# Weighted values of an even and an odd head issued alternately, each in its own half of the TensorE columns

## The chip, the cores and the metric

The program runs on one core of a Trainium2 chip. The metric is the device time of one execution in microseconds; the kernel before was timed three times. One further execution was taken with the hardware profiler, and all rows below are from that one. TensorE is called PE in the rows (PEld is its weight load), VectorE DVE, ScalarE ACT, GpSimd POOL, and SP is the engine that issues the DMAs.

## The reference

Two layers work on 256 tokens of width 1024. Each layer normalises, projects to a wide row (queries, keys and values of four mixers, gates, merge weights), runs four causal mixers with four heads of 64 each, merges their outputs through gates, and adds one output projection. Cut to what matters here:

```python
def _hybrid_layer(x, norm_w, w_in, cmp_pos, cmp_w1, cmp_w2, w_up, w_out):
    h = _rmsnorm(x, norm_w)
    proj = jnp.einsum('bsd,dc->bsc', h, w_in)
    ...
    o_a = _moba_attention(...)             # 4 heads, causal softmax over 256 keys
    o_b = _nsa_attention(...)              # 4 heads, three branches: compressed, selected, window
    o_c = _stick_breaking_attention(...)   # 4 heads, stick-breaking weights
    o_d = _dilated_attention(...)          # 12 heads in 3 groups, combined to 4
    widened = jnp.stack([_merge_heads(o_a) * jax.nn.silu(ga), ...], axis=2)
    u = jnp.einsum('bsiw,iwd->bsid', widened, w_up)
    y = jnp.sum(jax.nn.sigmoid(merge) * u, axis=2)
    return x + y @ w_out
```

With 256 tokens, MoBA's own block and the selected and the window branch all come to full causal attention. Each head ends in the same step: a matrix of weights (256 queries by up to 256 keys) times a matrix of values (256 keys by 64).

## The kernel before

Every projection is an fp32 product made of three fp32r products (high and low parts of activations and weights), so PE runs long rows of `pp<-hh,wh`, `pp<-hl,wh`, `pp<-hh,wl` with 256 moving columns. ACT makes the high part of each half of a weight (`wh`, a cast), DVE the low part (`wl`, a subtraction); the halves arrive by DMA in five `raw` buffers, and six `wh` and `wl` buffers hold them until PE has used them.

The order of all instructions is written out by a planner at build time. It goes through a list of items (T and N: projections, W1: the compressor's hidden layer, M and U: merge gates and up-projections), and between them it puts steps of the attention generators wherever its own clock says that their operands are ready (`fill`, `when`, `my_turn`, `turn`). At most three generators are open (`MAXA`). The branches come in the order a, c, b, d (`ORDER = (0, 2, 1, 3)`), the heads of a branch 0 to 3. The order on each engine is fixed by that; on the chip every engine works strictly through its own list and waits on semaphores.

One head goes as follows. Scores (`psS`, fp32r products with all 128 rows of the array) are read by DVE, softmaxed by ACT and DVE into `p` (for d: `pd`), and `transpose_P` (line 895) transposes the weights in three 128 by 128 pieces on PE into `psT`, from where ACT or DVE copies them to a buffer of the ring `ptr` (five buffers). Then come the products of this step, `mm_PV` (line 903): values are stationary (128 rows by 64 columns), transposed weights move. An even head writes partitions 0 to 63 of `psO`, an odd head partitions 64 to 127; heads 0 and 1 use the first half of the bank, heads 2 and 3 the second. One call is a product with 256 moving columns for the first 128 keys and one with 128 for the other keys. Heads of a and c make one call, heads of d three, heads of b two and one more product of 256 columns (`vct` and `pct`, the compressed branch). These products are plain fp32: the trace shows each as two records. After head 3, `close_branch` multiplies `psO` by the gate into `wid`, and then ACT and DVE split it into `widh` and `widl` for the U items.

Other products that use a part of the array's columns are those of the W1 items: four products with 32 stationary columns each, written one behind the other to the four quarters of the partitions, fp32 with 256 moving columns (`pp<-raw,xt` and `pp<-raw,qkv`; `xt` and `qkv` are buffers lent from the same ring).

The planner's price of a matmul whose output does not begin at partition 0 is `return 0.055` (line 165), and so it has been for every product of an odd head.

Of the kernel before, what the change touches and what calls it, by code (L numbers as in the profile page):

```python
# [189 lines left out]
def kernel(ctx: ExitStack, tc: tile.TileContext, x_in, w_half, w_kvb, w_up, norm_w, pe_in,  # L190
# [46 lines left out]
    ss = sb("ss", [128, 2, 5])  # L237
    rstd = sb("rstd", [128, 2])
    ms = sb("ms", [128, 2])
    pc = sb("pc", [128, 2, 4, 32])  # L240
    sg = sb("sg", [128, 2, 12])
    kct = sb("kct", [128, 2, 16])
    junk = sb("junk", [128, 1])
# [12 lines left out]
    for t in (hh[1], hl[1]):  # L256
        blk.put(t[:, 0:4, :])
        blk.put(t[:, 4:8, :])
    ptr = Ring("ptr", 5, [128, 384])
    tm = Ring("tm", 2, [128, 2, S])  # L260
    small = Ring("small", 10, [128, 16])

# [5 lines left out]
    done = set()  # L268
# [516 lines left out]
    def cmp_branch(l, h_):  # L785
        hc = h_[0:64, 0:256]
        u = p1.get()
        t_ = u[0:64, 0:256]
        nc.scalar.activation(out=t_, in_=hc, func=AF.Square)
        vec.tensor_scalar(out=t_, in0=t_, scalar1=0.044715, scalar2=1.0, op0=ALU.mult, op1=ALU.add)  # L790
        vec.tensor_tensor(out=t_, in0=t_, in1=hc, op=ALU.mult)
        act(out=t_, in_=t_, func=AF.Tanh, scale=0.7978845608028654)
        vec.scalar_tensor_tensor(out=t_, in0=t_, scalar=1.0, in1=hc, op0=ALU.add, op1=ALU.mult)
        p1.put(h_)
        yield when(u, ring=psT)
        b = rot(psT)
        for k in range(2):
            nc.tensor.transpose(b[:, 64 * k:64 * k + 64], u[0:64, 128 * k:128 * k + 128], iden[0:64, 0:64])
        gtk = u[:, 0:32].rearrange("p (k c) -> p k c", k=2)
        gtv = u[:, 32:288].rearrange("p (k h c) -> p k h c", k=2, h=4)  # L800
        bv = b[:, 0:128].rearrange("p (k c) -> p k c", k=2)
        act(out=gtk, in_=bv[:, :, 0:16], func=AF.Copy, scale=0.5)
        act(out=gtv, in_=bv[:, :, 32:64].unsqueeze(2).to_broadcast([128, 2, 4, 32]), func=AF.Copy, scale=0.5)
        yield when(gtk, gtv, ring=psT)
        b = rot(psT)
        for k in range(2):
            mm(b[:, 0:16], w2k[:, k, :], gtk[:, k, :], start=(k == 0), stop=(k == 1))
        for k in range(2):
            mm(b[:, 64:128], gtv[:, k].rearrange("p a b -> p (a b)"), w2v[:, k, :], start=(k == 0), stop=(k == 1))
        p1.put(u)  # L810
        nc.scalar.copy(kct[0:64, 0, :], b[0:64, 0:16])
        vec.tensor_copy(kct[64:128, 1, :], b[64:128, 0:16])
        for h in range(4):
            copy_to(vct[32 * h:32 * h + 32, h, :], b[32 * h:32 * h + 32, 64:128])
        while (l, "bq") not in done:
            yield cond((l, "bq"))
        yield when(kct, vct, T_[l, "bqr"], ring=psS)
        q = T_[l, "bqr"]
        b = rot(psS)
        for tt in range(2):  # L820
            for p in range(2):
                mm(b[:, 64 * tt + 32 * p:64 * tt + 32 * p + 32], q[:, 256 * p + 128 * tt:256 * p + 128 * tt + 128],
                   kct.rearrange("p a n -> p (a n)"), start=True, stop=True)
        t = p1.get()
        tv = t[:, 0:128].rearrange("p (a h n) -> p a h n", a=2, h=4)
        t8 = t[:, 0:128].rearrange("p (g n) -> p g n", n=16)
        m1, m2 = small.get(), small.get()
        vec.tensor_tensor(out=tv, in0=b[:, 0:128].rearrange("p (a h n) -> p a h n", a=2, h=4),
                          in1=cmask[:, 0].unsqueeze(2).to_broadcast([128, 2, 4, 16]), op=ALU.add)
        vec.tensor_reduce(out=m1[:, 0:8], in_=t8, op=ALU.max, axis=mybir.AxisListType.X)  # L830
        vec.tensor_tensor(out=t8, in0=t8, in1=m1[:, 0:8].unsqueeze(2).to_broadcast([128, 8, 16]), op=ALU.subtract)
        act(out=t[:, 0:128], in_=t[:, 0:128], func=AF.Exp, scale=0.125)
        qkv.put(q)
        while (l, "bkv") not in done:
            yield cond((l, "bkv"))
        vec.tensor_tensor(out=tv, in0=tv, in1=cmask[:, 1].unsqueeze(2).to_broadcast([128, 2, 4, 16]), op=ALU.mult)
        vec.tensor_reduce(out=m1[:, 0:8], in_=t8, op=ALU.add, axis=mybir.AxisListType.X)
        vec.tensor_scalar(out=m1[:, 0:8], in0=m1[:, 0:8], scalar1=1e-30, scalar2=None, op0=ALU.max)
        vec.reciprocal(out=m2[:, 0:8], in_=m1[:, 0:8])
        m2v = m2[:, 0:8].rearrange("p (a h) -> p a h", a=2)  # L840
        vec.tensor_tensor(out=m2v, in0=m2v, in1=sg[:, :, 0:4], op=ALU.mult)
        vec.tensor_tensor(out=pc[:, :, :, 0:16], in0=tv, in1=m2v.unsqueeze(3).to_broadcast([128, 2, 4, 16]), op=ALU.mult)
        p1.put(t)
        small.put(m1)
        small.put(m2)
        yield when(pc, ring=psT)
        b = rot(psT)
        for tt in range(2):
            nc.tensor.transpose(b[:, 128 * tt:128 * tt + 128], pc[:, tt].rearrange("p h n -> p (h n)"), iden)
        nc.scalar.copy(pct, b[:, 0:256])  # L850
        done.add((l, "cmp"))

# [47 lines left out]
        copy_to(t, b[:, 0:384])  # L900
        return t

    def mm_PV(h, v0, v1, pt, start, stop):
        r, p = 64 * (h % 2), h // 2
        mm(psO[r:r + 64, p, :], v0, pt[:, 0:256], start=start, stop=False)
        mm(psO[r:r + 64, p, 128:256], v1, pt[:, 256:384], start=False, stop=stop)

    def close_branch(l, i, scale):
        vec.scalar_tensor_tensor(out=wid[i].rearrange("p a b -> p (a b)"), in0=psO.rearrange("p a b -> p (a b)"),
# [9 lines left out]
            yield cond((l, "pv", i, h))  # L919

    def finish_head(l, i, h, scale, last):
        done.add((l, "pv", i, h + 1))
        if h == 3:
            done.add((l, "pvs", i))
            gn = (l, "g" + "abcd"[i])
            while gn not in done:
                yield cond(gn)
            yield when(psO)
            close_branch(l, i, scale)
            if last is not None:  # L930
                done.add((l, "pv", last, 0))
# [3 lines left out]
    def head_a(l, h):  # L935
        q, k, v = T_[l, "aq"], T_[l, "ak"], T_[l, "av"]
        b = mm_S(q, k, h)
        if h == 3:
            blk.put(q), blk.put(k[0]), kl.put(k[1])
        p, acc = p1.get(), small.get()  # L940
        score(b, p, 0, 0, acc, True)
        softmax(p, 1, acc)
        yield my_turn((l, 0, h), 1, p)
        pt = transpose_P(p, 0)
        seq["next"] += 1
        p1.put(p)
        small.put(acc)
        yield when(pt)
        yield from turn(l, 0, h)
        mm_PV(h, vslice(v, 0, 64 * h), vslice(v, 1, 64 * h), pt, True, True)  # L950
        ptr.put(pt)
        if h == 3:
            qkv.put(v)
        yield from finish_head(l, 0, h, 1.0, NEXT[0])

    def head_b(l, h):
        q, k, v = T_[l, "bq"], T_[l, "bk"], T_[l, "bv"]
        r = 64 * (h % 2)
        ps, accs = [], []
        b = mm_S2(q, k, h)  # L960
        if h == 3:
            blk.put(q), blk.put(k)
        for s in range(2):
            p, acc = p1.get(), small.get()
            score(b[s], p, 0, 0, acc, True)
            softmax(p, 1, acc, gate=sg[:, :, 4 * (s + 1) + h])
            ps.append(p)
            accs.append(acc)
        pts = []
        for s in range(2):  # L970
            yield my_turn((l, 1, h), 2 - s, ps[s])
            pts.append(transpose_P(ps[s], 0))
            p1.put(ps[s])
            small.put(accs[s])
        seq["next"] += 1
        yield when(*pts)
        while (l, "cmp") not in done:
            yield cond((l, "cmp"))
        yield from turn(l, 1, h)
        mm(psO[r:r + 64, h // 2, :], vct[:, h, :], pct, start=True, stop=False)  # L980
        for s in range(2):

            mm_PV(h, v[:, 64 * s:64 * s + 64], v[:, 128 + 64 * s:128 + 64 * s + 64], pts[s], False, s == 1)
            ptr.put(pts[s])
        if h == 3:
            qkv.put(v)
        yield from finish_head(l, 1, h, 1.0, NEXT[1])

    def head_c(l, h):
# [19 lines left out]
        pt = transpose_P(t, 0)  # L1009
        seq["next"] += 1  # L1010
        p1.put(t)
        yield when(pt)
        yield from turn(l, 2, h)
        mm_PV(h, vslice(v, 0, 64 * h), vslice(v, 1, 64 * h), pt, True, True)
        ptr.put(pt)
        if h == 3:
            qkv.put(v)
        yield from finish_head(l, 2, h, 0.5, NEXT[2])
# [16 lines left out]
    def head_d(l, h):  # L1035
# [6 lines left out]
        seq["next"] += 1  # L1042
        pd.put(p)
        small.put(acc)
        yield when(*pts)
        yield from turn(l, 3, h)
        for g in range(3):
            v = T_[l, f"dv{g}"]
            mm_PV(h, vslice(v, 0, 64 * h), vslice(v, 1, 64 * h), pts[g], g == 0, g == 2)
            ptr.put(pts[g])  # L1050
        if h == 3:
            for g in range(3):
                qkv.put(T_[l, f"dv{g}"])
# [184 lines left out]
    with tc.manual_schedule():  # L1238
# [59 lines left out]
        for t in kl.free:  # L1298
            for e in range(2):
                nc.gpsimd.memset(t[64 - 64 * e:128 - 64 * e, e::2, :].bitcast(F32), 0.0)  # L1300
        nc.gpsimd.memset(pc, 0.0)
        nc.gpsimd.memset(kct, 0.0)
        nc.gpsimd.memset(vct, 0.0)
        h0 = 0
# [167 lines left out]
```

## Time and profile before

| what | value |
|---|---|
| median of 3 runs | 658.98 us (658.93 to 659.08) |
| the profiled execution, its own time | 659.2 us |
| its span, first to last instruction | 657.3 us |
| PE busy | 639.6 us, 97% |
| PEld busy | 606.5 us, 92% |
| DVE busy | 482.8 us, 73% |
| ACT busy | 369.4 us, 56% |
| instructions | 12885 |

The profiled execution's time is 1.9 us longer than its span. Busy time of PE is the union of its records; records overlap, since a matmul of 256 columns is given some 0.28 us and the next one starts 0.12 us after it, so the pace of PE is read from starts.

### The profile page before, as it was taken

How to read it: one execution, taken by the hardware profiler on the slowest of the kernel's cores; microseconds unless marked ns; L12 is line 12 of the kernel's file. 1: busy time of each engine (PE TensorE's matmuls, PEld its weight loads, DVE VectorE, ACT ScalarE, POOL GpSimd, SP SyncE). 2: the span in 40 equal slices, each digit the busy share in tenths (PEclk: the TensorE clock that was granted, in tenths of full speed). 3: DMA queues.
4: the chain of work that ended last, by engine and by line, in shares of the span. 5: the costliest groups of instructions: out<-in, count | busy, mean ns of one | idle time of the engine just before them, and what ended most of it. 6: DMA issues, size and time to landing. Idle time of an engine off the chain costs nothing.

```text
span 657.3 us, 12885 instructions
## 1 busy us (share of the span) xinstructions
PE 639.6 (97%) x5192; PEld 606.5 (92%) x5192; DVE 482.8 (73%) x851; ACT 369.4 (56%) x656; POOL 46.5 (7%) x58
## 2 busy tenths in 40 slices
PE   7999999999999999999999999999999999999996
PEld 6998999999999999999999889899999989999996
DVE  6777788999974664667678678888999556555773
ACT  6546634545656777445464564545464757765452
POOL 3020100121100000000001101020220000000000
PEclk7999999999999999999999999999999999999998
DMA  8933255644443444567656144556336334345811
GB/s 286 330 131 123 102 203 216 234 151 145 164 159 97 147 159 137 182 243 240 215 178 232 59 166 157 186 205 224 132 128 207 132 138 146 117 153 198 290 63 65
DMA packets 34908, 112.38 MB, mean 171 GB/s; under 512 B 4257, under 2 KB 5281, under 8 KB 34849
## 3 DMA queue, kind: packets, MB, share of 16 engines
q1 hardware_dynamic: 34560, 111.07, 49.0%
q0 software_dynamic: 144, 0.49, 0.4%
q8 instruction: 41, 0.67, 0.4%
q14 instruction: 19, 0.15, 0.1%
q10 hardware_dynamic: 144, 0.00, 0.0%
HBM read 109.94 MB, written 2.10 MB: 170 GB/s over the span
## 4 chain that ended last, share of the span: by engine, by line
PE 73%; DVE 17%; issue 4%; ACT 3%; DMA 2%; POOL 0%; SPq 0%; POOLq 0%; DVEq 0%; ACTq 0%
PE pp L149 60%; PE psO L149 7%; DVE wl L149 7%; DVE rope L149 4%; PE psT L149 3%; PE psS L149 3%; DMA raw<-w_half_dram 2%; DVE xt L149 2%; DVE hl L149 1%; ACT wh L149 1%; ACT p L149 1%; DVE pd L149 1%; DVE p L149 1%; ACT hh L149 1%; DVE hh L149 0%
## 5 line engine op out<-in xcount | busy, mean ns | idle before, releaser
L149 PE MATMUL pp<-hh,wh 128*128 128x256 f32 x1008 | 290.0, 288 | 1.5 <-DVE xt L149 1.5
L149 PE MATMUL pp<-hh,wl 128*128 128x256 f32 x1008 | 282.6, 280 | 2.3 <-DVE wl L149 2.3
L149 PE MATMUL pp<-hl,wh 128*128 128x256 f32 x1008 | 282.4, 280 | 0.0
L149 DVE TENSOR_TENSOR wl<-raw,wh 128x1024 fp32r<-128x1024 f32 (+2 forms) x198 | 232.1, 1190 | 51.2 <-ACT wh L149 50.3
L149 ACT CAST wh<-raw 128x1024 fp32r<-128x1024 f32 (+2 forms) x198 | 188.7, 978 | 51.7 <-DMA raw<-w_half_dram 28.0
L149 PEld LDWEIGHTS pp<-hh,wh 128*128 128x128 f32 x1008 | 190.0, 188 | 10.0 <-issue 6.5
L149 PEld LDWEIGHTS pp<-hh,wl 128*128 128x128 f32 x1008 | 190.0, 188 | 3.2 <-DVE wl L149 3.2
L149 PEld LDWEIGHTS pp<-hl,wh 128*128 128x128 f32 x1008 | 189.9, 188 | 0.2
L149 PE MATMUL pp<-wh,hh 128*128 128x256 f32 (+1 forms) x320 | 86.1, 289 | 1.1 <-ACT hh L149 1.1
L149 PE MATMUL pp<-wl,hh 128*128 128x256 f32 (+1 forms) x320 | 83.9, 281 | 1.4 <-DVE wl L149 1.4
L149 PE MATMUL pp<-wh,hl 128*128 128x256 f32 (+1 forms) x320 | 84.3, 284 | 0.0
L149 ACT ACTIVATE p<-p,small 128x128 f32<-128x128 f32 x96 | 40.0, 448 | 38.4 <-DVE small L149 37.7
L149 PEld LDWEIGHTS pp<-wh,hh 128*128 128x128 f32 x320 | 58.8, 193 | 2.4 <-ACT hh L149 1.6
L149 PEld LDWEIGHTS pp<-wl,hh 128*128 128x128 f32 x320 | 57.6, 188 | 1.8 <-DVE wl L149 1.8
L149 PEld LDWEIGHTS pp<-wh,hl 128*128 128x128 f32 x320 | 58.2, 191 | 0.0
L149 DVE TENSOR_TENSOR rope<-pp,sinF 32x512 f32<-32x512 f32 x72 | 49.5, 687 | 6.6 <-PE pp L149 4.0
L149 POOL TENSOR_TENSOR xt<-xt,rope 128x512 f32<-128x512 f32 x14 | 28.1, 2005 | 172.2 <-DVE xt L149 140.0
L149 PE MATMUL psO<-ptr,xt 128*64 128x256 f32 x192 | 37.7, 332 | 0.0
L149 PE MATMUL pp<-widh,wh 128*128 128x256 f32 x128 | 36.5, 285 | 0.0
L149 PE MATMUL pp<-widh,wl 128*128 128x256 f32 x128 | 35.8, 280 | 0.0
L149 PE MATMUL pp<-widl,wh 128*128 128x256 f32 x128 | 35.8, 279 | 0.0
L149 ACT COPY ptr<-psT 128x384 f32<-128x384 f32 x46 | 21.2, 477 | 24.1 <-PE psT L149 24.0
(146 smaller groups left out, 688.0 us busy)
## 6 DMA issues: line engine op xcount, KB each, us to landing
raw<-w_half_dram SPq DMA_DIRECT2D x178, 512.0 KB, 4.3
raw<-w_up_dram SPq DMA_DIRECT2D x32, 256.0 KB, 3.1
raw<-w_kvb_dram SPq DMA_DIRECT2D x4, 536.0 KB, 5.6
xt<-x_in_dram SPq DMA_DIRECT2D x4, 256.0 KB, 3.2
xt<-x_in_dram SPq DMA_DIRECT2D x2, 512.0 KB, 7.3
pd<-norm_w_dram SPq DMA_DIRECT2D x2, 512.0 KB, 6.1
x_mem<-xt SPq DMA_DIRECT2D x2, 512.0 KB, 5.2
xt<-x_mem SPq DMA_DIRECT2D x2, 512.0 KB, 5.6
```

What stands on the lines that cost most here:

```text
L149: return f(*a, **k)
```

## The change

The scores are not touched. `mm_PV` becomes a generator: the even head only leaves its list of products and its `ptr` buffers in `held`; the odd head waits until the transposed weights of both are there and then issues both lists in turns, one product of the even head (partitions 0 to 63), one of the odd (64 to 127). The products themselves, their number and their operands stay. The `ptr` buffers of both heads go back after that, the ring has six of them in place of five, and room for the sixth comes from the tile `pc`, whose values now lie in a `p1` buffer, cleared by a memset in each layer in place of one at the start.

```diff
-    pc = sb("pc", [128, 2, 4, 32])
...
-    ptr = Ring("ptr", 5, [128, 384])
+    ptr = Ring("ptr", 6, [128, 384])
...
         t = p1.get()
+        pc = t[:, 128:384].rearrange("p (a h n) -> p a h n", a=2, h=4)
+        nc.gpsimd.memset(pc[:, :, :, 16:32], 0.0)
...
-        p1.put(t)
...
             nc.tensor.transpose(b[:, 128 * tt:128 * tt + 128], pc[:, tt].rearrange("p h n -> p (h n)"), iden)
+        p1.put(t)
...
-    def mm_PV(h, v0, v1, pt, start, stop):
-        r, p = 64 * (h % 2), h // 2
-        mm(psO[r:r + 64, p, :], v0, pt[:, 0:256], start=start, stop=False)
-        mm(psO[r:r + 64, p, 128:256], v1, pt[:, 256:384], start=False, stop=stop)
+    held = {}
+
+    def pv(v0, v1, pt):
+
+        return [(0, v0, pt[:, 0:256]), (128, v1, pt[:, 256:384])]
+
+    def mm_PV(l, i, h, steps, pts):
+
+        held[l, i, h] = steps, pts
+        if h % 2 == 0:
+            return
+        a, b = held.pop((l, i, h - 1)), held.pop((l, i, h))
+        yield when(*a[1], *b[1])
+        yield from turn(l, i, h - 1)
+        n = len(a[0])
+        for k in range(n):
+            for r, (st, _) in ((0, a), (64, b)):
+                c, v, p = st[k]
+                mm(psO[r:r + 64, h // 2, c:256], v, p, start=(k == 0), stop=(k == n - 1))
+        for _, pts in (a, b):
+            for pt in pts:
+                if pt is not pct:
+                    ptr.put(pt)
...
     def finish_head(l, i, h, scale, last):
-        done.add((l, "pv", i, h + 1))
+        if h % 2:
+            done.add((l, "pv", i, h + 1))
...
-        yield when(pt)
-        yield from turn(l, 0, h)
-        mm_PV(h, vslice(v, 0, 64 * h), vslice(v, 1, 64 * h), pt, True, True)
-        ptr.put(pt)
+        yield from mm_PV(l, 0, h, pv(vslice(v, 0, 64 * h), vslice(v, 1, 64 * h), pt), [pt])
...
-        mm(psO[r:r + 64, h // 2, :], vct[:, h, :], pct, start=True, stop=False)
+        steps = [(0, vct[:, h, :], pct)]
...
+            steps += pv(v[:, 64 * s:64 * s + 64], v[:, 128 + 64 * s:128 + 64 * s + 64], pts[s])
+        yield from mm_PV(l, 1, h, steps, [pct] + pts)
...
-            mm_PV(h, vslice(v, 0, 64 * h), vslice(v, 1, 64 * h), pts[g], g == 0, g == 2)
-            ptr.put(pts[g])
+            steps += pv(vslice(v, 0, 64 * h), vslice(v, 1, 64 * h), pts[g])
+        yield from mm_PV(l, 3, h, steps, pts)
...
-        nc.gpsimd.memset(pc, 0.0)
```

Since the planner sets the order, all engines' lists change. The numbers behind the names are the buffer and the tile, and a tile's number is smaller by one after the change for what is allocated behind `pc`. On PE, in layer 0, this is the second head of branch a before, with the projection around it; the products of head 0 (`ptr0_138`) stand 45 rows higher in the list, by themselves:

```order
L149 MATMUL pp1_156<-hh0_78,wh3_105 128x256
L149 MATMUL pp1_156<-hl0_80,wh3_105 128x256
L149 MATMUL pp1_156<-hh0_78,wl3_111 128x256
L149 MATMUL psO_162<-ptr1_139,xt_77 64x256
L149 MATMUL psO_162<-ptr1_139,xt_77 64x128
L149 MATMUL pp1_156<-hh0_78,wh3_105 128x256
L149 MATMUL pp1_156<-hl0_80,wh3_105 128x256
```

At the same place of the list after the change:

```order
L149 MATMUL pp1_156<-hh0_78,wh3_104 128x256
L149 MATMUL pp1_156<-hl0_80,wh3_104 128x256
L149 MATMUL pp1_156<-hh0_78,wl3_110 128x256
L149 MATMUL psO_162<-ptr0_137,xt_77 64x256
L149 MATMUL psO_162<-ptr1_138,xt_77 64x256
L149 MATMUL psO_162<-ptr0_137,xt_77 64x128
L149 MATMUL psO_162<-ptr1_138,xt_77 64x128
L149 MATMUL pp1_156<-hh0_78,wh4_105 128x256
L149 MATMUL pp1_156<-hl0_80,wh4_105 128x256
```

The products of both heads now stand in one place and take turns, and the projection is interrupted once in place of twice.

On PE, in layer 0, this is the first head of branch d before; behind it come 57 other rows and then the six products of head 1 in the same form:

```order
L149 MATMUL psO_162<-ptr1_139,xt_77 64x256
L149 MATMUL psO_162<-ptr1_139,xt_77 64x128
L149 MATMUL psO_162<-ptr2_140,xt_77 64x256
L149 MATMUL psO_162<-ptr2_140,xt_77 64x128
L149 MATMUL psO_162<-ptr3_141,qkv0_114 64x256
L149 MATMUL psO_162<-ptr3_141,qkv0_114 64x128
```

After the change the first two heads of d stand together:

```order
L149 MATMUL psO_162<-ptr4_141,xt_77 64x256
L149 MATMUL psO_162<-ptr1_138,xt_77 64x256
L149 MATMUL psO_162<-ptr4_141,xt_77 64x128
L149 MATMUL psO_162<-ptr1_138,xt_77 64x128
L149 MATMUL psO_162<-ptr5_142,xt_77 64x256
L149 MATMUL psO_162<-ptr2_139,xt_77 64x256
L149 MATMUL psO_162<-ptr5_142,xt_77 64x128
L149 MATMUL psO_162<-ptr2_139,xt_77 64x128
L149 MATMUL psO_162<-ptr0_137,qkv0_113 64x256
L149 MATMUL psO_162<-ptr3_140,qkv0_113 64x256
L149 MATMUL psO_162<-ptr0_137,qkv0_113 64x128
L149 MATMUL psO_162<-ptr3_140,qkv0_113 64x128
```

All six `ptr` buffers are in use here, three of each head, and no weights of head 2 are transposed until these rows are through.

On DVE the list of layer 0 is almost the same as before up to the branch b, and that of layer 1 differs most where branch a ends and branch c begins. Before, the first head of c (`p14`, `p13`, its scores and scans) stands ahead of the subtractions `wl5` and `wl0` and of the closing of branch a (`wid0_82<-psO`):

```order
L149 TENSOR_TENSOR wl4_112<-raw2_99,wh4_106 128x1024
L149 TENSOR_TENSOR p14_130<-psS1_159,masks_70 128x128
L149 TENSOR_TENSOR p14_130<-psS1_159,masks_70 128x256
L149 TENSOR_SCALAR p12_128<-p14_130 128x384
L149 SCALAR_TENSOR_TENSOR p13_129<-p12_128,zero_76 128x128
L149 SCALAR_TENSOR_TENSOR p13_129<-p12_128,zero_76 128x256
L149 SCALAR_TENSOR_TENSOR p14_130<-p14_130,p13_129 128x128
L149 SCALAR_TENSOR_TENSOR p14_130<-p14_130,p13_129 128x256
L149 TENSOR_TENSOR wl5_113<-raw4_101,wh5_107 128x1024
L149 TENSOR_TENSOR wl0_108<-raw0_97,wh0_102 128x1024
L149 SCALAR_TENSOR_TENSOR wid0_82<-rope0_124,pp1_156 128x512
L149 SCALAR_TENSOR_TENSOR wid0_82<-psO_162,wid0_82 128x512
```

After the change:

```order
L149 TENSOR_TENSOR wl5_112<-raw4_100,wh5_106 128x1024
L149 SCALAR_TENSOR_TENSOR wid0_82<-rope0_123,pp1_156 128x512
L149 SCALAR_TENSOR_TENSOR wid0_82<-psO_162,wid0_82 128x512
L149 TENSOR_TENSOR wl0_107<-raw0_96,wh0_101 128x1024
L149 TENSOR_TENSOR widl_87<-wid0_82,widh_86 128x512
L149 TENSOR_TENSOR hh1_79<-qkv2_115,hh1_79 64x2x256 x2
L149 TENSOR_TENSOR wl1_108<-raw3_99,wh1_102 128x1024
L149 SCALAR_TENSOR_TENSOR wid1_83<-rope1_124,pp0_155 128x512
L149 TENSOR_TENSOR p14_129<-psS1_159,masks_70 128x128
L149 TENSOR_TENSOR p14_129<-psS1_159,masks_70 128x256
L149 TENSOR_SCALAR p12_127<-p14_129 128x384
```

The head of c has moved behind three subtractions and the closing of branch a.

## Rows read from the trace of the kernel before

**Rows 1.** The page: busy times, PE's granted clock in 40 slices, the chain by line.
```profile
PE 639.6 (97%) x5192; PEld 606.5 (92%) x5192; DVE 482.8 (73%) x851; ACT 369.4 (56%) x656; POOL 46.5 (7%) x58
PEclk7999999999999999999999999999999999999998
PE pp L149 60%; PE psO L149 7%; DVE wl L149 7%; DVE rope L149 4%; PE psT L149 3%; PE psS L149 3%; DMA raw<-w_half_dram 2%; DVE xt L149 2%; DVE hl L149 1%; ACT wh L149 1%; ACT p L149 1%; DVE pd L149 1%; DVE p L149 1%; ACT hh L149 1%; DVE hh L149 0%
```
**Rows 2.** PE's timeline around one head of a: start us, us, what.
```profile
64.06 0.28 PE L149 MATMUL pp<-hh,wl 128*128 128x256 f32 x1
64.27 0.86 PE L149 MATMUL psO<-ptr,xt 128*64 128x256 f32 x4
65.06 0.38 PE L149 MATMUL pp<-hh,wh 128*128 128x256 f32 x1
65.28 0.27 PE L149 MATMUL pp<-hl,wh 128*128 128x256 f32 x1
65.40 0.28 PE L149 MATMUL pp<-hh,wl 128*128 128x256 f32 x1
```
**Rows 3.** The chain in order of time: start us, us, what.
```profile
64.34 0.80 PE psO L149 x4
...
197.47 1.88 PE psO L149 x10
...
243.40 2.10 PE psO L149 x12
...
270.07 58.03 PE pp L149 x492
```
**Rows 4.** PE's timeline of two W1 items in a row, and the row behind.
```profile
91.89 0.40 PE L149 MATMUL pp<-raw,xt 128*32 128x256 f32 x1
...
91.91 0.40 PE L149 MATMUL pp<-raw,qkv 128*32 128x256 f32 x1
92.13 0.38 PE L149 MATMUL pp<-raw,xt 128*32 128x256 f32 x1
...
92.34 0.38 PE L149 MATMUL pp<-raw,xt 128*32 128x256 f32 x1
...
92.89 0.39 PE L149 MATMUL pp<-hh,wh 128*128 128x256 f32 x1
```
**Rows 5.** The timeline of PE's weight loads, another W1 item.
```profile
60.56 0.11 PEld L149 LDWEIGHTS pp<-raw,xt 128*32 128x32 f32 x1
...
60.61 0.11 PEld L149 LDWEIGHTS pp<-raw,qkv 128*32 128x32 f32 x1
```
**Rows 6.** The instructions on `psO`: duration ns min/median/max, first and last start.
```profile
L149 PEld LDWEIGHTS psO<-ptr,xt x192: 132/137/137, 57.7 to 589.2; 128*64 128x64 f32 x192
```
**Rows 7.** DVE's timeline where branches a and c run, in brackets the idle time.
```profile
89.28 1.23 DVE L149 TENSOR_TENSOR wl<-raw,wh 128x1024 fp32r<-128x1024 f32 x1 [1.24 <-ACT wh L149]
...
100.75 0.62 DVE L149 TENSOR_TENSOR p<-psS,masks 128x128 f32<-128x128 f32 x2 [1.04 <-PE psS L149]
...
110.05 2.08 DVE L149 TENSOR_TENSOR rope<-pp,sinF 32x512 f32<-32x512 f32 x3 [1.55 <-PE pp L149]
```
**Rows 8.** Busy us by stretch: PE, PEld, DVE, ACT, POOL, clock, DMA share, GB/s.
```profile
110.00:170.00 60.00, 58.00 (x490) 55.53 (x489) 56.98 (x94) 31.75 (x49) 11.32 (x6) 1.00 0.47 162
195.00:270.00 75.00, 75.00 (x579) 68.50 (x577) 43.60 (x85) 53.03 (x108) 0.00 (x0) 1.00 0.41 134
```
**Rows 9.** DVE's timeline among the heads of b.
```profile
212.92 1.22 DVE L149 TENSOR_TENSOR wl<-raw,wh 128x1024 fp32r<-128x1024 f32 x1
```
**Rows 10.** PE's timeline, the first use of what that subtraction made.
```profile
214.65 0.28 PE L149 MATMUL pp<-hh,wl 128*128 128x256 f32 x1
```
**Rows 11.** The copies of transposed weights: duration ns min/median/max.
```profile
L149 ACT COPY ptr<-psT x46: 460/479/487, 57.1 to 585.0; 128x384 f32<-128x384 f32 x46
...
L149 DVE COPY ptr<-psT x10: 548/558/561, 63.2 to 586.8; 128x384 f32<-128x384 f32 x10
```
**Rows 12.** PE's longest waits: us in total, times, longest.
```profile
PE pp L149 <- DVE wl L149: 3.8, 5, 1.1
```

More of the change, by code (lines that the diff above doesn't have):

```diff
@@ L957, in head_b @@
         q, k, v = T_[l, "bq"], T_[l, "bk"], T_[l, "bv"]
-        r = 64 * (h % 2)
         ps, accs = [], []
@@ L975, in head_b @@
         seq["next"] += 1
-        yield when(*pts)
         while (l, "cmp") not in done:
             yield cond((l, "cmp"))
-        yield from turn(l, 1, h)
-        mm(psO[r:r + 64, h // 2, :], vct[:, h, :], pct, start=True, stop=False)
+        steps = [(0, vct[:, h, :], pct)]
         for s in range(2):
-            mm_PV(h, v[:, 64 * s:64 * s + 64], v[:, 128 + 64 * s:128 + 64 * s + 64], pts[s], False, s == 1)
-            ptr.put(pts[s])
+            steps += pv(v[:, 64 * s:64 * s + 64], v[:, 128 + 64 * s:128 + 64 * s + 64], pts[s])
+        yield from mm_PV(l, 1, h, steps, [pct] + pts)
         if h == 3:
@@ L1011, in head_c @@
         p1.put(t)
[L1012 to L1015, printed above, removed]
+        yield from mm_PV(l, 2, h, pv(vslice(v, 0, 64 * h), vslice(v, 1, 64 * h), pt), [pt])
         if h == 3:
@@ L1044, in head_d @@
         small.put(acc)
-        yield when(*pts)
-        yield from turn(l, 3, h)
+        steps = []
         for g in range(3):
             v = T_[l, f"dv{g}"]
-            mm_PV(h, vslice(v, 0, 64 * h), vslice(v, 1, 64 * h), pts[g], g == 0, g == 2)
-            ptr.put(pts[g])
+            steps += pv(vslice(v, 0, 64 * h), vslice(v, 1, 64 * h), pts[g])
+        yield from mm_PV(l, 3, h, steps, pts)
         if h == 3:
```

## The prediction

> **What bounds the kernel now.** I read the page first [rows 1]: PE is busy for 97% of the span, its granted clock stands at the full 2.4 GHz in every slice but the first and the last, and on the chain that ended last the projections (`pp`) hold 60% and the products on `psO` 7%, which is 46 us of 657.3. DVE's groups are second, some 16% together. So I looked for two things: what a product on `psO` costs PE, and where DVE and not PE sets the pace.
>
> PE's records overlap, so I take its pace from starts. In the long undisturbed run at 270 us, 492 projection records fill 58.03 us, 0.118 us each [rows 3]. Around a head of a, the last projection record ahead starts at 64.06 and the second one behind at 65.28 [rows 2]: 1.22 us where two steps of the pace would be 0.24. **One head of a or c costs PE 0.98 us.** On the chain its products hold 0.80 us; a head of b holds 1.88 and one of d 2.10 [rows 3]. With the same surroundings b costs 0.98 + 1.08 = 2.06 us and d 0.98 + 1.30 = 2.28 us. From d less a, (2.10 - 0.80) / 2 = 0.65 us, comes the price of one product of 256 moving columns with its fellow of 128, and two thirds of that, 0.43 us, for the one of 256. So 0.33 us of each head is no product at all: it is the step into half an array and back, seen as the late first starts in [rows 2]. All heads together: 16 x 0.98 + 8 x 2.06 + 8 x 2.28 = 50.4 us.
>
> **The change part by part.** *Products in turns.* Instructions and operands stay; what can change is whether the two halves of the columns work at the same time. The kernel has a row for it. In the W1 items four products with 32 stationary columns and the same 256 moving columns start at 91.89 to 91.91, and the next four at 92.34 [rows 4]: four in 0.45 us, where one alone is 0.43 and four in a row would be 1.7. They have four different moving operands and all 128 rows, as the products here. Two halves of 64 columns are that case with two parts, so a pair should cost what one head costs now, and one head of each pair goes: 8 x 0.98 + 4 x 2.06 + 4 x 2.28 = 25.2 us.
>
> Not all of it: four side by side took 0.45 where one takes 0.43. At 0.02 us a product, with 2, 5 and 6 products in the pairs, that is 8 x 0.04 + 4 x 0.10 + 4 x 0.12 = 1.2 us; if only the start of the second is later, 0.01 us a pair, 0.1 us. I take 0.5.
>
> *Weight loads.* Each record loads 64 columns, 0.137 us at the median [rows 6], twice as many per time as now. In a W1 item eight loads, for both passes of four products, start between 60.56 and 60.61 [rows 5], and the first matmul, 0.40 us long [rows 4], runs from the start of this: loads do not wait for it, though all have the same 128 rows. I price this at nothing. The Trainium skill, "TensorE: Matmul & The Clock Gate", section Part 3: Packing small matmuls — row/col tiling, says otherwise: a weight load would overlap with a running matmul only where the row groups differ, and here they are the same. By that rule this change would give much less (the third rival below has it in numbers of this trace); the W1 rows contradict it, since their row groups are the same too.
>
> *How much of it the end of the kernel sees.* A shorter PE counts where PE sets the pace. Among a and c (50 to 110 us, and again in layer 1) PE gains 4 x 0.98 = 3.9 us a layer, but the stretch behind, 110 to 170 us, is DVE's: 56.98 of 60 us busy [rows 8], and PE's largest wait in the whole trace is for `wl` [rows 12]. That stretch only moves up as far as DVE begins it earlier. Ahead of it DVE stood idle for PE 1.04 us and 1.55 us [rows 7]; these 2.6 us can go. The 1.24 us at 89.28 wait for a cast, and it is open whether that comes earlier. So 2.6 to 3.9 us a layer remain; I take the middle, 3.2, since the cast's buffers are released partly by PE.
>
> Among b and d (195 to 270 us) PE gains 2 x 2.06 + 2 x 2.28 = 8.7 us a layer. DVE is busy for 43.60 of 75 us and ACT for 53.03 [rows 8]; in 66.3 us ACT would be at 80%, so neither becomes the bound. Here the covers are single ones: a `wl` that ends at 212.92 + 1.22 = 214.14 us [rows 9] is first used at 214.65 [rows 10], 0.51 us later, when PE will be a head of b, 2.06 us, earlier. If DVE came no earlier there, 1.55 us would be lost. The remainder is between 7.1 and 8.7 us a layer; I take 8.0, since DVE itself waits for PE in this stretch and will mostly move along.
>
> *The later wait.* The even head's products now wait for the odd head's weights too, and on PE everything behind them is queued. Between the last transposes and the products the new list has at least six projection rows, 0.7 us, for a copy of 0.48 or 0.56 us [rows 11]. Behind a subtraction of 1.22 us [rows 9] DVE's copy would end 1.1 us late, but the head of [rows 2] has the same distance in the list of before, and nothing but the step of every head stands ahead of it. Nothing, then; at two such places a layer 4 us at most, for the range.
>
> *Sixth buffer, `pc`.* The buffer frees the planner to transpose all of a pair of d. A smaller memset moves from the start into each layer's 110 to 170 us, on POOL, with 11.32 of 60 us busy [rows 8]; the rope addition behind it could come later by the length of a memset, which no row has. POOL's 48 idle us hide it. The `p1` buffer that `pc` borrows is held a little longer. Nothing for both. In layer 1 the first head of c stands later on DVE, behind subtractions that it would have to do anyway; I price that at nothing too, with 1 us either way.
>
> **Sum.** 2 x (3.2 + 8.0) - 0.5 = 21.9 us. The profiled execution took 659.2 us, 0.2 above the median of the three runs, so 637.3 for such an execution and **637.1 us** for the median.
>
> **Rivals.**
> 1. *All of it arrives* (DVE moves along everywhere, and waits for `wl` shrink in the new order): 659.0 - 25.2 + 0.1 = 633.9, perhaps 1 us less. For it: DVE's idle time ahead of 110 us is largely made by PE. Against it: 95% busy behind. Chance 0.13, for anything under 634.5.
> 2. *DVE keeps more*: nothing of a and c arrives, and b and d keep 7.1 us: 659.0 - 14.2 + 0.5 = 645.3. For it: the 110 to 170 us stretch; against it: the 2.6 us that PE made. Chance 0.14 for 641 to 648.
> 3. *The loads of the odd half wait.* Odd heads have 4 records in a and c, 10 in b, 12 in d: 8 x 4 + 4 x 10 + 4 x 12 = 120 records, each with 0.137 us outside: 16.4 us of 25.2 are lost, and with the same share of what is left arriving (21.9 of 25.2), 659.0 - 7.6 = 651.4. It is what the section named above would make of it; [rows 5] speak against it. Chance 0.03.
> 4. *The change doesn't do what it says*: halves of 64 columns take turns and don't overlap. Then only 16 steps into and out of the half array go, 16 x 0.33 = 5.3 us: 653.7. Only W1 with quarters speaks against it. Chance 0.03.
> 5. *Slower.* PE stands before a pair whose odd weights are not copied, and everything queues behind. To be slower by over 0.2% this must eat 21.9 + 1.3 us, 1.45 us at each of the 16 pairs; the worst that I made of a subtraction ahead of a copy is 1.1, at the tightest places. Chance 0.01.
>
> The forecast, 634.5 to 641, has 0.66. Its own range is that; the range for 8 in 10 takes in most of the first rival and the nearer part of the second, **633 to 644**. A difference of 0.2%, 1.3 us, is about what the runs can tell from none. Faster 0.98 (all but the fifth and a sliver), same 0.01, slower 0.01.
>
> **What would show it.** Records of `psO` start in twos, some ns apart, at the pace of one head: 0.8 us for a pair of a or c, 1.9 for b, 2.1 to 2.2 for d; on the chain `psO` falls from 7% to under 4%, and PE is busy for about 617 us. In the stretch that was 110 to 170, DVE stays over 90% busy and PE's waits for `wl` grow from 3.8 to some 5 us. Between b and d no wait of PE is over 1 us. The prediction is wrong if the second record of a pair starts 0.1 us or more behind the first, if PE waits in front of `psO`, or if DVE's stretch ends no earlier than now.

## The result, and the profile after

The changed kernel takes 638.18 us (median, 637.66 to 639.46) where the kernel before takes 658.95 in the same session: a ratio of 0.9685, 95% interval 0.967 to 0.9701. That is 20.8 us less; predicted were 637.1 us, with 633 to 644 as the range. The profiled execution took 637.66 us with a span of 635.8; that is 0.5 us below its median, and before it was 0.2 us above, so the two profiled executions lie 0.8 us further apart than the medians.

The page, its busy times and the chain by line, which answer to [rows 1]:

```profile
PE 616.4 (97%) x5192; PEld 591.8 (93%) x5192; DVE 482.2 (76%) x850; ACT 369.3 (58%) x657; POOL 46.4 (7%) x59
PE pp L149 58%; DVE wl L149 7%; DVE rope L149 4%; PE psO L149 3%; PE psT L149 3%; ACT p L149 3%; PE psS L149 3%; ACT wh L149 2%; DVE xt L149 2%; DMA raw<-w_half_dram 2%; DVE hl L149 1%; DVE p L149 1%; DVE pd L149 1%; DVE kl L149 1%; DVE qkv
```

PE has as many instructions as before and 23.2 us less busy time; `psO` has gone from 7% to 3% of the chain. PE's timeline around the first pair of a (start us, us, what), where [rows 2] had one head:

```profile
63.75 0.28 PE L149 MATMUL pp<-hh,wl 128*128 128x256 f32 x1
63.96 0.87 PE L149 MATMUL psO<-ptr,xt 128*64 128x256 f32 x8
64.76 0.39 PE L149 MATMUL pp<-hh,wh 128*128 128x256 f32 x1
64.98 0.28 PE L149 MATMUL pp<-hl,wh 128*128 128x256 f32 x1
```

Eight records stand where four stood, and the projection resumes 0.80 us after they begin, as it did behind one head (0.79 in [rows 2]). The eight start in twos, each second record 7 ns behind the first, and their weight loads keep up:

```profile
63.96 0.63 PEld L149 LDWEIGHTS psO<-ptr,xt 128*64 128x64 f32 x8
```

The chain in order of time shows the same for all three kinds; these are pairs, with the durations that single heads have in [rows 3]:

```profile
64.03 0.80 PE psO L149 x8
...
202.47 1.88 PE psO L149 x20
...
237.07 2.10 PE psO L149 x24
```

PE's waits (us in total, times, longest), beside [rows 12]:

```profile
PE pp L149 <- DVE wl L149: 4.3, 5, 1.6
PE pp L149 <- DVE xt L149: 1.7, 2, 1.0
PE psO L149 <- DVE p L149: 1.5, 1, 1.5
...
PE pp L149 <- DVE widl L149: 0.9, 2, 0.5
```

The wait for `widl` is new; the one of `psO` for `p` is on eight records at the very start and as long before the change. Busy time by stretch, as in [rows 8], shows DVE still setting the pace from 110 to 170 us:

```profile
110.00:170.00 60.00, 58.05 (x491) 55.58 (x490) 57.20 (x99) 33.84 (x52) 11.85 (x7) 1.00 0.49 166
195.00:270.00 75.00, 74.50 (x645) 70.95 (x643) 47.00 (x81) 55.73 (x109) 0.00 (x0) 1.00 0.47 159
```

Where the time was gained is read from the projection's records: their number is the same in all kernels here, so the start of the k-th tells how far PE is ahead of the kernel before. The starts in us (W1 not counted):

| record, and what ends there | before | after | ahead | gained in the stretch |
|---|---|---|---|---|
| 1200, a and c of layer 0 and the stretch behind | 188.92 | 184.72 | 4.20 | 4.20 |
| 2400, b and d of layer 0 | 358.64 | 346.79 | 11.85 | 7.65 |
| 3360, a and c of layer 1 | 505.70 | 491.56 | 14.14 | 2.29 |
| 4320, b and d of layer 1 | 645.32 | 623.76 | 21.56 | 7.42 |

### The profile page after: what moved, and what is told of

Its sections match the earlier page's. It is cut to its first block, busy times and chain, and to the rows that moved or that the text cites. A ratio compares the mean times of both kernels' runs of the same rounds, so it can differ in the third digit from the quotient of the medians.

```text
span 635.8 us, 12881 instructions
## 1 busy us (share of the span) xinstructions
PE 616.4 (97%) x5192; PEld 591.8 (93%) x5192; DVE 482.2 (76%) x850; ACT 369.3 (58%) x657; POOL 46.4 (7%) x59
## 4 chain that ended last, share of the span: by engine, by line
PE 67%; DVE 19%; ACT 6%; issue 4%; DMA 2%; POOL 0%; SPq 0%; POOLq 0%; ACTq 0%; DVEq 0%
PE pp L149 58%; DVE wl L149 7%; DVE rope L149 4%; PE psO L149 3%; PE psT L149 3%; ACT p L149 3%; PE psS L149 3%; ACT wh L149 2%; DVE xt L149 2%; DMA raw<-w_half_dram 2%; DVE hl L149 1%; DVE p L149 1%; DVE pd L149 1%; DVE kl L149 1%; DVE qkv L149 1%
## 5 line engine op out<-in xcount | busy, mean ns | idle before, releaser
L149 ACT ACTIVATE tm<-pp 128x512 f32<-128x512 f32 x32 | 19.0, 592 | 22.4 <-PE pp L149 22.4
```

The source lines that it names most:

```text
L149: return f(*a, **k)
```

## The experiments

**Even list, then odd list.** The same place and the same products, but one head behind the other:

```diff
-        for k in range(n):
-            for r, (st, _) in ((0, a), (64, b)):
+        for r, (st, _) in ((0, a), (64, b)):
+            for k in range(n):
```

> The products of a pair stay in one place of PE's list, but all of the even head stand ahead of all of the odd head. Theory (the halves work at the same time only where the matmuls of the two stand in turns, since PE starts matmuls in the order of its list): a pair costs the products of both heads, 0.65 + 0.65 us in a and c, 1.73 each in b, 1.95 each in d, and one step into the half array; that is 8 x 0.65 + 4 x 1.73 + 4 x 1.95 = 19.9 us more than with turns, less up to 0.2 us a pair where the last product of the one and the first of the other overlap and less what waits take up: 653 to 658 us. Rival (PE finds the other half's matmuls in its queue by itself, so that standing close is enough): 638 us, as with turns.

Measured: 648.56 us, ratio 0.9842 (0.9828 to 0.9856). Neither was right; half of the gain is left. PE's timeline of the first pair of b says why. In the list ten records of the even head (`vct`, then four products from `ptr`) stand ahead of the odd head's `vct`:

```profile
204.63 0.65 PE L149 MATMUL psO<-pct,vct 128*64 128x256 f32 x2
205.11 1.03 PE L149 MATMUL psO<-ptr,xt 128*64 128x256 f32 x5
205.77 0.43 PE L149 MATMUL psO<-pct,vct 128*64 128x256 f32 x1
205.98 0.38 PE L149 MATMUL psO<-ptr,xt 128*64 128x256 f32 x1
206.03 0.38 PE L149 MATMUL psO<-pct,vct 128*64 128x256 f32 x1
206.19 1.52 PE L149 MATMUL psO<-ptr,xt 128*64 128x128 f32 x10
207.64 0.73 PE L149 MATMUL psS<-hl,hh 128*128 128x256 f32 x3
```

The odd head's `vct` starts at 205.77, 6 ns after the seventh even record, with three even records still to start. In d it starts 6 ns after the ninth of twelve. So, by the starts that the profile shows, PE took up the odd half with four even records left, the one just begun and three to come: two fp32 products. It did not work strictly through its list here, as the section on the kernel before has it for every engine. The four records of a head of a lie within that, and there the pair is free without any turns. The chain of this kernel:

```profile
65.99 0.81 PE psO L149 x8
...
204.70 3.01 PE psO L149 x19
...
241.51 3.45 PE psO L149 x24
```

Against the change, 4 x (3.01 - 1.88) + 4 x (3.45 - 2.10) = 9.9 us, and 648.56 - 638.18 is 10.4.

**Both heads in the same half.** The lists and turns of the change, row for row, but the odd head writes the same partitions as the even one (prices held, so that the order stays):

```diff
-                mm(psO[r:r + 64, h // 2, c:256], v, p, start=(k == 0), stop=(k == n - 1))
...
+                u = 64 * (h // 2)
+                mm(psO[u:u + 64, r // 64, c:256], v, p, start=(k == 0 and r == 0), stop=(k == n - 1 and r == 64))
...
```

> List, turns and sizes as after the change on every engine, but both heads of a pair write to the same half of the partitions, next to each other in the bank (heads 0 and 1 below, 2 and 3 above), so that the output mixes the heads' columns; nothing is left out. Theory (what is gained is the two halves of the columns at work together): every product waits for the one ahead, 19.9 us more: 654 to 658 us, and the records of psO start 0.2 us apart in place of 7 ns. Rival (the gain is in the new order, fewer steps between full and half array, or a later place of the products): 638 to 641 us.

Measured: 657.68 us, ratio 0.9973 (0.996 to 0.9985). The theory holds, and the rival falls: the new order with half as many interruptions is worth 1 to 2 us. In the trace PE, DVE, ACT and POOL each start the same operations in the same order as in the change. Its chain:

```profile
63.93 1.44 PE psO L150 x8
...
205.22 3.61 PE psO L150 x20
...
243.31 4.04 PE psO L150 x24
```

8 x 0.64 + 4 x 1.73 + 4 x 1.94 = 19.8 us more than in the change; the medians differ by 19.5. Beside this run the lists one behind the other save 0.63, 0.60 and 0.59 us at a pair (1.44 - 0.81, 3.61 - 3.01, 4.04 - 3.45), however long the pair is. That is about the 0.65 us of the four records that were left when the odd half began.

**The parts that go with it.** The sixth `ptr` buffer with `pc` in a `p1` buffer, without the new `mm_PV`; and, in another kernel, the planner's price of an odd head's products at the full value (`return 0.055` not for `psO`).

> The kernel before with only the supporting edits: six buffers of transposed weights in place of five, and the compressed branch's weights in a borrowed buffer with a memset in each layer. Products head by head as before. Theory: no part of the gain, 658 to 660 us. Rival (the sixth buffer lets the planner issue transposes earlier and that is worth something by itself): 655 us or less.

> The kernel before with only the planner's price of an odd head's products set to that of an even head's (0.43 and 0.22 us in place of 0.055). Theory: the order changes but PE's work doesn't, 657 to 661 us. Rival (the kernel before lost time because its planner took odd heads for nearly free, and the change made that price true): a part of the 21 us comes back, 650 to 656 us.

Measured: 659.14 us, ratio 1.0004 (0.9993 to 1.0016), and 660.36 us, 1.0017 (1.0004 to 1.003). Neither has a part in the gain; the second is, if anything, 0.2% slower.

**Turns of two and of three products.** These test the reading that PE looks four records ahead (shown for two; for three the step is 3):

```diff
-        for k in range(n):
+        for k0 in range(0, n, 2):
             for r, (st, _) in ((0, a), (64, b)):
-                c, v, p = st[k]
+                for k in range(k0, min(k0 + 2, n)):
+                    c, v, p = st[k]
...
```

> The pairs take turns by two products in place of one. After the run with the heads in a row the theory is changed: PE starts a matmul for the free half while up to four records (two products of two records each) of the other half stand ahead of it, the one at work included, and no more. Two products are then no more than that: each pair costs 0.80, 1.88 and 2.10 us as with turns of one, 638 us, +-0.7. Rival (any departure from strict turns costs a part, because starts follow the list and only neighbours overlap): each further product in a row costs its 0.2 to 0.43 us somewhere, 641 to 647 us.

> Turns of three products; the pairs of a and c have two and so stand in a row, which cost nothing in the earlier run. By the changed theory the odd half of b and d starts when the third record of the even half starts, 0.48 us late, and ends as much later, with no further loss since the even half is ahead: 8 pairs x 0.5 = 4 us, less what waits take up, 640 to 642.5 us; in the records the first of the odd half 0.48 us behind the first of the even half. Rival (the look-ahead is no fixed number of records; b and d lost in the earlier run because their loads or the vct product come first): 638 us, or as with the heads in a row, 648 us.

Measured: 639.27 us, ratio 0.9685 (0.9663 to 0.9708), with two; 642.32 us, 0.9735 (0.9708 to 0.9761), with three. With two, the first odd record starts 13 ns behind the first even one, and pairs of b and d take 1.93 and 2.15 us. In b the four records ahead are then all of 256 columns, 0.86 us of work, where 0.65 us were left in the run with one list behind the other: it is the number of records that fits both, not a time. Records and products can't be told apart here, since every product is two records. With three, it starts 0.489 us behind, straight after the third even record at 0.483 and again with four left; the chain of that kernel:

```profile
64.58 0.81 PE psO L149 x8
...
203.21 2.36 PE psO L149 x17
...
238.72 2.58 PE psO L149 x19
```

That is 0.48 us more at each of eight pairs, 3.8 in all; the medians differ by 4.1 across two sessions. Against turns of two, in the same session, the pairs give 3.5 and the medians 3.05.

**Where the missing 3.6 us went.** The pairs give 25.2 us on PE (below), and 21.56 arrive. In layer 0 the whole of a and c is kept (4.20 of 3.9), in layer 1 only 2.29. There the planner opens branch c late: its last pair begins at 415.87 us, 42.9 us behind the layer's first pair, where layer 0 has 38.3. My reading is that DVE then reaches its subtractions late; PE waits longest at 475.68:

```profile
475.68 0.38 PE L149 MATMUL pp<-hh,wl 128*128 128x256 f32 x1 [1.62 <-DVE wl L149]
```

A head is opened only while the planner's clocks of ACT and DVE are less than `BACKLOG` ahead of PE's (no run shows that this is what held c back). So I raised that number in the changed kernel:

```diff
-BACKLOG = 1
+BACKLOG = 1.5
```

> After the change, but the planner may open a head when DVE and ACT are 1.5 us ahead in its clock in place of 1 (BACKLOG). By that the first head of c stands as early in layer 1 as in layer 0. Theory (1.6 us of a's and c's gain got lost in layer 1 since c came late there and its DVE work fell into the stretch that DVE sets): 636.3 to 637.4 us, and in layer 1 PE is 3.5 us or more ahead of before at the end of that stretch. Rival (DVE's work as such sets it, the order doesn't matter): 637.6 to 639 us.

Measured: 634.83 us, ratio 0.9627 (0.9601 to 0.9652), better than both kernels and than I had expected (3.4 us below the change by the medians, 2.8 by the two profiles). The last pair of c begins at 410.30 us, and of PE's waits (us in total, times, longest) the one for `wl` has shrunk:

```profile
PE pp L149 <- DVE wl L149: 2.6, 3, 1.1
```

The k-th records tell where: ahead of before by 3.75, 11.88, 16.24 and 24.35 us at the four places of the table, so 4.36 us are kept in layer 1's a and c, 2.07 more than in the change, 0.5 and 0.7 more among b and d of the two layers, and 0.45 less in layer 0's a and c. The number moves much else in the order, so this agrees with a late branch c as the cause, and doesn't single it out. But 24.35 of 25.2 us arrive here, so DVE's work as such is not what kept most of the missing 3.6.

**The planner's pace.** If a wrong clock were the cause, the true pace of a projection record should help as well:

```diff
-                return max(m, 256) * 0.000426
+                return max(m, 256) * 0.00046
```

> After the change, but the planner's price of an fp32r matmul is what the trace shows (0.118 us for 256 columns in place of 0.109). Theory (what PE still waits for is DVE's work and not the planner's clock): the order changes, the waits for wl move but keep their sum of some 4 us, 636.5 to 640 us. Rival (with the odd heads no longer late against the plan, the plan's fast clock is now what makes PE wait): 633.5 to 636 us.

Measured: 653.54 us, ratio 0.9902 (0.9882 to 0.9922), some 15 us worse than the change and far from both expectations. The loss is all among a and c: PE is 6.78 us behind the kernel before at record 1200 (195.69 us) and loses 5.34 in layer 1, while b and d gain 9.55 and 9.16. Its largest wait is for `wl`, and others are new:

```profile
PE pp L149 <- DVE wl L149: 5.8, 2, 2.9
PE psT L149 <- DVE qkv L149: 2.6, 3, 1.2
...
PE pp L149 <- DVE wid L149: 1.7, 2, 0.9
PE psS L149 <- DVE kct L149: 1.6, 2, 0.9
```

A wait here costs more than its length. PE's timeline at the longest, and the busy times around it in the form of [rows 8], with the granted clock as the third number from the end:

```profile
150.99 0.58 PE L149 MATMUL pp<-hh,wl 128*128 128x256 f32 x1 [2.92 <-DVE wl L149]
151.38 0.41 PE L149 MATMUL pp<-hh,wh 128*128 128x256 f32 x1
151.59 0.41 PE L149 MATMUL pp<-hl,wh 128*128 128x256 f32 x1
...
150.00:155.00 5.00, 4.01 (x22) 4.01 (x23) 4.51 (x7) 0.94 (x3) 2.21 (x2) 0.66 0.49 147
```

Behind the wait the projection records start 0.21 us apart in place of 0.12, so for a part of these 5 us the clock stood at 1.2 in place of 2.4 GHz. At 0.34 x 5 this is an estimated 1.7 us, and the stretch from 467 to 472 us, behind the other long wait for `wl`, shows 0.66 again.

That left open whether these numbers act on the change or on any order, so both went into the kernel before.

> The kernel before with one number of the planner changed as in the run that beat both kernels: a head may be opened while the planner's clocks of ACT and DVE are up to 1.5 us ahead of PE's, in place of 1. If the 3.3 us which that run gained over the changed kernel were taken back from a c branch that the change had made the planner open late, the kernel before has little of it to gain: 658 to 661 us, ratio 0.998 to 1.003. Rival: the number helps any order of this kernel, and the gain has nothing to do with the change: some 3 us faster than before, 655 to 656.5, ratio about 0.995.

> The kernel before with the planner's price of a product of 256 columns raised from 0.109 to 0.118 us, the edit that cost the changed kernel 15 us. If the loss is a matter of the planner alone (its clock of PE then runs later, it opens heads and gives PE waits elsewhere), the kernel before loses a like amount: 668 to 678 us, ratio 1.015 to 1.03. Rival: the loss needs the pairs of the changed kernel: within 3 us of before, 656 to 662.

Measured: 669.83 us, ratio 1.0158 (1.0132 to 1.0183), and 684.06 us, 1.0371 (1.0344 to 1.0398). In the first, theory and rival both fall: the number that gains 3.4 us in the changed kernel costs 10.4 in the kernel before, spread over all four stretches (behind by 1.70, 3.82, 5.90 and 8.57 us at the places of the table). In the second the direction of the theory holds, and the loss is larger than it gave, 24.6 us; over a third of it is a wait that no other kernel here has in that size, products on `psO` that wait for DVE to read the branch before out of it (PE's waits):

```profile
PE psO L149 <- DVE wid L149: 9.4, 2, 4.7
```

Here too the loss is among a and c (19.1 and 15.8 us lost there, 6.1 and 3.5 gained among b and d). The granted clock is 0.77 from 80 to 95 us and 0.83 from 415 to 425, around these two waits, an estimated 5.2 us more (0.23 x 15 and 0.17 x 10).

So a planner number shifts the end by 3 to 25 us through the order alone, with what the waits in it do to the granted clock. With equal numbers on both sides the change is still worth 0.9627 / 1.0158 = 0.948 and 0.9902 / 1.0371 = 0.955, beside 0.9685 as it stands.

## Why the prediction was right, step by step

**Halves overlap: right, and shown.** The place of the odd head's output alone moves 657.68 to 638.18 us. The fourth rival (halves take turns, 653.7) falls with that run and with the 7 ns.

**Loads of the odd half wait: not so.** The weight loads keep up with pairs 7 ns apart, and a pair takes what a head took. The rule of the Trainium skill that stands behind that rival ("TensorE: Matmul & The Clock Gate", Part 3: Packing small matmuls — row/col tiling), a load overlapping only where row groups differ, doesn't hold for these column halves. The same section of the Trainium skill has matmuls start strictly in the order of the list; in the run with one list behind the other, the record at 205.77 started ahead of three that stand before it.

**25.2 us gross: right.** From the first record to the next other one, the 32 heads take 44.47 us before (0.794, 1.876 and 2.094 each) and the 16 pairs 22.34 after. The late first starts around each saved group add 16 x 0.19 us (first record 0.21 us after the projection in place of 0.12, second projection record behind 0.22 in place of 0.12): 25.2. **The 0.5 us** that I took off for pairs was too much: a pair is 0.007 us longer than a head, 16 x 0.007 = 0.1. The quarters of W1 had misled a little.

**What the end sees: right in sum, off in its parts.** For a and c I kept 3.2 us a layer; 4.20 and 2.29 were kept, 6.5 in place of 6.4. That sum is luck: both lie outside the bounds of 2.6 to 3.9 that I gave, one on either side. In layer 0 DVE moved up with PE in full: from 50 us to the end of its stretch it is idle some 4 us less than before, also at places that I hadn't listed, as two waits for scores of 0.94 and 0.99 us at 67.26 and 77.41 us. For b and d I kept 8.0; it was 7.65 and 7.42, so 15.1 in place of 16.0, inside the bounds of 7.1 to 8.7. The cover that I named was not the one that failed most. A `wl` between two pairs of b cost 0.24 us at 217.79. The larger loss is at a `widl`; DVE's timeline and PE's there, start us, us, what:

```profile
200.87 0.69 DVE L149 TENSOR_TENSOR widl<-wid,widh 128x512 fp32r<-128x512 f32 x1
...
200.92 0.28 PE L149 MATMUL pp<-widh,wh 128*128 128x256 f32 x1
201.61 0.38 PE L149 MATMUL pp<-widl,wh 128*128 128x256 f32 x1 [0.41 <-DVE widl L149]
```

Before, the products of b's head 0 (1.88 us, at 197.47 in [rows 3]) stood on PE ahead of this U item. Now they wait for head 1, and the pair comes at 202.4 us, behind it; the cover is gone. From 200.92 to 201.61 is 0.69 us where the pace is 0.12, so 0.57 are lost, and 0.64 at the same place of layer 1 (511.96). With the `wl` there and in layer 1 (at 528.25), 0.24 and 0.27 us, that is 1.7 of the 2.3 us that are missing from 2 x 8.7; the rest I did not trace.

**Priced at nothing.** The sixth buffer, `pc` and the odd heads' price: right, by the two runs on them. The later wait for the odd copies: right; PE waits before no pair. The new order in layer 1, "1 us either way", is **the step that was not sound**: layer 1's a and c kept 0.9 us less than my 3.2, which is within that 1 us, but 2.07 less than in the run with the larger backlog, and the planner's numbers show that order alone can cost 10 to 25 us. I had looked at the lists for a wait, but had bounded the effect by nothing.

**The signs that I named.** Twos some ns apart, 0.80, 1.88 and 2.10 us, 3% of the chain, 616.4 us busy, 57.20 of 60 us on DVE, no wait over 1 us between b and d, none before a pair: all there. PE's waits for `wl` grew to 4.3, not to 5.

**Still open.** Which of the planner's decisions cost the 15 us with the true pace, and most of the 10 us of the larger backlog in the kernel before, was not settled. In the profiles PE stands idle 9.5 us more with the true pace than in the change, of 15.4 us in the spans, and the clock takes an estimated 3.4; in the kernel before it is 16.1 and 5.2, of 25.5. Why the planner's order has these waits stays open.

## What to carry to other kernels

Small products that fill half of TensorE's columns were worth pairing with products for the other half: the pair cost what one cost. But the list has to bring the partner soon, since here it was taken up no more than four records ahead. Price the pairing by a place in the same trace where it already happens, and take out the part that another engine's stretch keeps. Where a planner writes the order, compare the two kernels under more than one of its settings: the change was worth 3.2% to 5.2% depending on a number that has nothing to do with it.

## What the runs showed of the hardware

- TensorE ran two streams of fp32 products with 64 stationary columns each, in different halves of its columns and on all 128 rows, with starts 7 ns apart; a pair took 0.007 us longer than one list. The granted clock was 1.00 of 2.4 GHz in both stretches shown.
- It started an odd-half record ahead of even-half records listed before it, always with four of these left (the one just begun included): after the seventh of ten, the ninth of twelve, the third of six. If four or fewer stood ahead, the odd one started 13 ns behind the first.
- Two heads in the same half, with the same turns, took 1.44 us where two halves took 0.80.
- Behind a wait of 2.9 us PE's granted clock was 0.66 over 5 us, with projection records 0.21 us apart in place of 0.12.
